# A two-layer decoder with routed experts on one core: another opening of the first expert products

## The chip, the core and the metric

The kernel runs on one core of one Trainium2 chip. TensorE (PE) multiplies, VectorE (DVE), ScalarE (ACT) and GpSimd (POOL) work element by element, SyncE (SP) and the queues of ScalarE and GpSimd issue DMAs. Every engine takes its instructions in the order in which they stand in the program; between engines, semaphores make one wait for another. The metric is the time of one execution on the device in microseconds (us); lower is better.

## What is computed

There are two layers over 256 tokens of width 1024. Each mixes tokens (attention in windows, a short convolution, a spatial gate) and then sends every token through PEER, a mixture of 128 x 128 experts of one neuron each. Only the second half matters here:

```python
q = (t @ w_pq).reshape(T, PEER_HEADS, 2, PEER_HALF)
s = jnp.einsum('thpk,hpnk->thpn', q, sub_keys)
top_s, top_i = lax.top_k(s, PEER_TOPK)                # 16 of 128 keys, twice for each of 8 heads
cand_s = top_s[:, :, 0, :, None] + top_s[:, :, 1, None, :]
best_s, best_pos = lax.top_k(cand_s.reshape(T, PEER_HEADS, 256), PEER_TOPK)
experts = jnp.take_along_axis(cand_i.reshape(T, PEER_HEADS, 256), best_pos, axis=-1)
gate = jax.nn.softmax(best_s, axis=-1)
act = jax.nn.gelu(jnp.einsum('td,thkd->thk', t, expert_down[experts]))
return jnp.einsum('thk,thkd->td', gate * act, expert_up[experts])
```

A token thus chooses 8 x 16 = 128 of 16384 experts.

## The kernel before, and its profile in words of the code

**Two ways to the same result.** The first T tokens of a layer (DENSE: 168 in layer 0, 160 in layer 1) are computed densely: each of 128 chunks of `down` (512 KB, 128 x 1024 f32) is multiplied with all T tokens on TensorE, the result goes through Gelu and is weighted with a gate matrix that is zero but for the chosen experts; then 128 chunks of `up` are multiplied and summed. The last 256 - T tokens (88 and 96) are computed by rows: for each token one indirect DMA from GpSimd's queue (`fetch`, L1038) gathers its 128 rows of `down` (512 KB again), VectorE multiplies them with the token (`dot`, L1048), and later the same is done with its rows of `up` (`add_row`, L1063). Rows are laid out by sets of tokens: 64, 16 and 8 tokens in layer 0, 64 and 32 in layer 1; each set needs the expert numbers and the token's values spread over the partitions (`spread_picks` into `pairs`, `dot_spread` into R_DX), and `where` (L1030, VectorE) turns the spread numbers into row addresses.

**The first products.** `experts` runs a loop over the 128 `down` chunks, numbered from 0. In the same loop stand, by a budget per chunk (`run_fill`), the steps of the choice on VectorE. They come for two halves of 128 tokens: first half 1 (tokens 128 to 255, which holds the tokens computed by rows), then half 0. The steps of a half are top-16 of the keys (`top_keys`), candidate sums (`cand`), top-16 of these (`top_cand`), `ranks`, three steps that turn positions into key numbers (`match`, `times`, `total`), `gate` (the softmax, with its Exp on ScalarE) and for half 1 `choose`, which writes `chosen`. When a half is known, `to_picks` transposes its results on TensorE (L918) and copies them on. The chunk at which half 1 is known is `begin` (11 in layer 0); the spreads and `where` are put at fixed lags behind it. After the second picks, `start`, the gate matrices are made (`compare` on VectorE, `factors` on ScalarE, `gate_mm` on TensorE).

**Buffers.** Chunks go through a ring of 7 buffers (`raw`), sent half by SP and half by ScalarE's queue. Ten chunks of a layer (AHEAD_AT) are sent early to free places of a large array (`arena`). Six more buffers hold chunks of the next modulation matrix (`aside`), which VectorE multiplies between other work. A row fetch needs a free place too: some fixed ones, and the seven of PASSING, which held early chunks before and are given up (`retired`) when the choice of half 0 nears its end, since results will lie there. Every `dot` frees the place of its row and fetches the next. DOT_SLOW and DOT_RATE are dots per chunk, before and after `start`. All DMAs of GpSimd's queue use eight semaphores in turn, so that one waits for the landing of the eighth before it.

**Lines.** L345 is a chunk's matmul of the first products, L1137 of the second, L1143 adds the rows' sums; L918 transposes picks, L926 copies them; L905 is the Exp, L906 to L908 the rest of the gate; L1020 and L1025 are the spreads.

Of the kernel before, what the change touches and what calls it, by code (L numbers as in the profile page):

```python
# [77 lines left out]
def hybrid_trunk(ctx: ExitStack, tc: tile.TileContext, x_in, c_in, vec_in, w_ada, w_in, w_out, w_pq,  # L78
# [37 lines left out]
    for n, t in enumerate(DENSE):  # L116
        for off, m in token_sets(S - t):
            nc.vector.tensor_reduce(fold[n][:, off:off + m], ident.rearrange("p (g n) -> p n g", n=m), op=OP.add,
                                    axis=AX.X)
    x_dram = dram.tile([P, DC * S], F32, name="x_dram")  # L120
# [39 lines left out]
    SLOTS_OPEN = [region(at * S, D) for at in (96, 100, 104)]  # L160
# [22 lines left out]
    class Src:  # L183
# [6 lines left out]
        asides = deque()  # L190
        ring = []
# [25 lines left out]
    def ada_chunk(layer, col, raw):  # L217
# [3 lines left out]
        if layer == 0 and col < G1:  # L221
            n = 1
        if (col + 1) % n == 0:
# [7 lines left out]
    def load_more(k):  # L231
        while Src.loaded < len(Src.seq) and (Src.ring[Src.loaded + 1] == Src.ring[Src.loaded]
# [75 lines left out]
    for layer in range(DEPTH):  # L308
# [3 lines left out]
        if layer == 0:  # L312
# [8 lines left out]
            body += mix(tail[:6], ada(0, [5])) + tail[6:]  # L321
        else:
            body += tail
# [8 lines left out]
        un = mix(un, aside[len(ASIDES_AT[layer]):], 4, 100)  # L332
# [490 lines left out]
    def retrieval(layer, update, late):  # L823
# [21 lines left out]
        tmp = R_PK[:, 3:6, :]  # L845
        sel = R_PK[:, 6:9, :]
# [6 lines left out]
        narrowed = R_TE[:, 0, 0].rearrange("p j i k -> p (j i k)")[:, :256].rearrange("p (h j i) -> p h j i", h=8, j=2)  # L853
# [47 lines left out]
        def gate():  # L901
# [3 lines left out]
            nc.scalar.activation(sel[:, 2, :], sel[:, 2, :], AF.Exp)  # L905
            nc.vector.tensor_reduce(red[:, :8], g, op=OP.add, axis=AX.X)  # L906
# [8 lines left out]
        def to_picks(b):  # L915
            ps = bank("g", 2)
            for j in range(3):
# [4 lines left out]
            high = tmp[:, 0, :].bitcast(F16)[:, :P]  # L922
# [30 lines left out]
        for d in range(DC):  # L953
            nc.scalar.activation(R_HX[:, d, :], R_H[:, d, :], AF.Identity, bias=shifts[:, d:d + 1])
        for pair in range(1, 8):
# [8 lines left out]
        def rest():  # L964
            scores(7)
            for b in (1, 0):
# [423 lines left out]
```

## Time and profile before

| what | value |
| --- | --- |
| three runs, median (lowest to highest) | 1617.16 us (1615.1 to 1618.89) |
| the profiled execution, its span | 1619.4 us, 1617.7 us |
| TensorE, VectorE, ScalarE, GpSimd busy | 96%, 62%, 29%, 32% |
| moved by DMA, mean rate | 570.27 MB, 353 GB/s |
| row fetches (L1038), all four forms | 368 |
| placing of sets by GpSimd, L1025 and L1020 | 32 and 32 DMAs |

The profile is one execution. A row of its views gives an engine, a line of the kernel, an operation, what it writes and reads, and in brackets how long the engine stood idle before it and what ended that. A row of the table by windows gives, for a stretch of time, the busy time of each engine with its count of instructions, TensorE's granted clock, the share of the DMA engines that was busy, and the GB/s that they moved. A chunk's product is 16 records of matmul in the profile, eight instructions in the program.

### The profile page before, as it was taken

The numbers are of one execution on the slowest core, as the hardware profiler recorded it, in microseconds if no ns is written. First come the engines' busy times: TensorE is split into PE (matmuls) and PEld (weight loads), VectorE is DVE, ScalarE is ACT, GpSimd is POOL, SyncE is SP. The second block draws the span as 40 slices with busy tenths as digits, with TensorE's granted clock in tenths as the row PEclk, the third lists the DMA queues.
The fourth block names the chain that finished last, engine by engine and source line by source line (L and its number), as shares of the span: only waits on it lengthen the run. The fifth ranks groups of instructions, "written<-read, shape, count | busy, mean of one in ns | idle before, by whom it ended". The sixth has DMA issues, their size and how long they took to land.

```text
span 1617.7 us, 29030 instructions
## 1 busy us (share of the span) xinstructions
PE 1550.2 (96%) x11240; PEld 1514.8 (94%) x11240; DVE 1002.7 (62%) x2263; ACT 475.4 (29%) x1356; POOL 518.5 (32%) x467
## 2 busy tenths in 40 slices
PE   7999996999999999998979999989999999999996
PEld 6879996999999999998979899989999999999995
DVE  6778884777777444444436668859777754444435
ACT  2346311466654000000015763115655510000000
POOL 1000125533333544444400001145433444444441
PEclk9999998999999999999979999989999999999997
DMA  9998647999999999999955666499999999999995
GB/s 387 344 361 310 184 151 254 360 419 418 419 418 418 418 419 419 418 419 418 420 216 169 195 231 198 149 387 374 419 418 418 418 419 419 419 419 418 418 419 201
DMA packets 157082, 570.27 MB, mean 353 GB/s; under 512 B 18736, under 2 KB 19312, under 8 KB 155792
## 3 DMA queue, kind: packets, MB, share of 16 engines
q1 hardware_dynamic: 65232, 237.92, 38.4%
q0 software_dynamic: 56144, 201.41, 31.3%
q10 hardware_dynamic: 35568, 129.08, 20.2%
q8 instruction: 88, 1.44, 0.3%
q14 instruction: 50, 0.41, 0.1%
HBM read 562.39 MB, written 3.15 MB: 350 GB/s over the span
## 4 chain that ended last, share of the span: by engine, by line
DMA 41%; PE 35%; issue 11%; POOL 6%; DVE 4%; ACT 2%; POOLq 0%; ACTq 0%; SPq 0%; DVEq 0%
DMA arena<-in_up,arena 28%; PE ch L345 18%; DMA spots<-in_up,arena 6%; POOL arena L1038 5%; DMA arena<-in_down_rows,arena 4%; PE ch L347 2%; PE ch L348 2%; PE ch L349 2%; DMA spots<-in_down_rows,arena 1%; DMA raw<-in_w_ada 1%; PE acc L1143 1%; POOL spots L1038 1%; DVE spots L1063 1%; PE ch L434 1%; PE g L936 1%
## 5 line engine op out<-in xcount | busy, mean ns | idle before, releaser
L345 PE MATMUL ch<-arena,raw 128*128 128x168 f32 (+2 forms) x3936 | 590.1, 309 | 8.2 <-issue 6.3
L1137 PE MATMUL acc<-arena,raw 128*128 128x168 f32 (+1 forms) x4096 | 581.0, 305 | 9.0 <-DMA raw<-in_up 9.0
L1137 PEld LDWEIGHTS acc<-arena,raw 128*128 128x128 f32 x4096 | 578.4, 192 | 11.0 <-DMA raw<-in_up 10.9
L345 PEld LDWEIGHTS ch<-arena,raw 128*128 128x128 f32 x3936 | 563.9, 192 | 15.5 <-issue 9.6
L1063 DVE SCALAR_TENSOR_TENSOR spots<-arena,spots 128x1024 f32<-128x1024 f32 x157 | 201.6, 1284 | 264.0 <-DMA arena<-in_up,arena 263.6
L1038 POOL DMA_INDIRECT arena<-in_up,arena x159 | 220.7, 1388 | 276.6 <-DMA arena<-in_up,arena 222.5
L1038 POOL DMA_INDIRECT arena<-in_down_rows,arena x148 | 163.1, 1102 | 240.1 <-DVE arena L1048 212.5
L1048 DVE SCALAR_TENSOR_TENSOR arena<-arena,spots 128x1024 f32<-128x1024 f32 x148 | 179.8, 1222 | 92.4 <-DMA arena<-in_down_rows,arena 90.7
L1081 ACT ACTIVATE arena<-arena,parts 128x128 f16<-128x128 f16 x164 | 64.6, 394 | 121.5 <-DVE arena L1071 81.2
L1114 ACT ACTIVATE arena<-ch 128x320 f32<-128x320 f32 (+30 forms) x122 | 42.0, 344 | 167.6 <-PE ch L345 141.7
L376 ACT ACT_TABLE_LOAD x6 | 7.7, 1283 | 264.5 <-PE acc L1137 264.4
L347 PE MATMUL ch<-hh,hi 128*128 128x256 f32 x288 | 82.6, 289 | 2.0 <-DVE arena L465 1.9
L348 PE MATMUL ch<-hh,lo 128*128 128x256 f32 x288 | 81.8, 284 | 0.0
L349 PE MATMUL ch<-hh,hi 128*128 128x256 f32 x288 | 81.7, 284 | 0.0
L258 DVE TENSOR_TENSOR lo<-raw,hi 128x1024 fp32r<-128x1024 f32 x42 | 51.2, 1224 | 24.0 <-ACT hi L265 23.8
L1038 POOL DMA_INDIRECT spots<-in_down_rows,arena x36 | 43.9, 1218 | 67.0 <-DVE spots L1048 47.9
L345 PE MATMUL ch<-arena 128*128 128x160 f32 (+2 forms) x384 | 62.7, 323 | 1.7 <-ACT arena L398 1.5
L218 DVE SCALAR_TENSOR_TENSOR raw<-raw,arena 128x1024 f32<-128x1024 f32 x48 | 57.8, 1215 | 9.1 <-DMA raw<-in_w_ada 5.5
L1087 ACT ACTIVATE arena<-arena,parts 128x128 f16<-128x128 f16 x164 | 63.4, 387 | 0.0
L1083 ACT ACTIVATE arena<-arena,parts 128x128 f16<-128x128 f16 x164 | 63.4, 387 | 0.0
L1085 ACT ACTIVATE arena<-arena,parts 128x128 f16<-128x128 f16 x164 | 63.4, 387 | 0.0
L345 PEld LDWEIGHTS ch<-arena 128*128 128x128 f32 x384 | 57.8, 194 | 6.0 <-ACT arena L398 4.0
(227 smaller groups left out, 1716.7 us busy)
## 6 DMA issues: line engine op xcount, KB each, us to landing
raw<-in_up SPq DMA_DIRECT2D x128, 512.0 KB
raw<-in_up ACTq DMA_DIRECT2D x128, 512.0 KB
raw<-in_down SPq DMA_DIRECT2D x118, 512.0 KB
raw<-in_down ACTq DMA_DIRECT2D x118, 512.0 KB
raw<-in_w_ada SPq DMA_DIRECT2D x48, 512.0 KB
aside<-in_w_ada SPq DMA_DIRECT2D x48, 512.0 KB
raw<-in_w_pq SPq DMA_DIRECT2D x32, 512.0 KB
raw<-in_w_in SPq DMA_DIRECT2D x26, 512.0 KB
```

Source lines behind the costliest of these rows:

```text
L345: nc.tensor.matmul(dst, hi[:, cols], k[0], start=start, stop=stop, **kw)
L347: nc.tensor.matmul(dst, hi[:, cols], k[0], start=start, stop=False, **kw)
L348: nc.tensor.matmul(dst, lo[:, cols], k[0], start=False, stop=False, **kw)
L349: nc.tensor.matmul(dst, hi[:, cols], k[1], start=False, stop=stop, **kw)
L1038: nc.gpsimd.indirect_dma_start(out=held[n], out_offset=None, in_=rows if n >= TS else down_rows[:, :], in_offset=bass.IndirectOffsetOnAxis ...
L1048: nc.vector.scalar_tensor_tensor(row, row, 1.0, R_DX[which(k)[0]], op0=OP.mult, op1=OP.mult, accum_out=R_DOTS[:, k:k + 1])
L1063: nc.vector.scalar_tensor_tensor(R_SUM[s], row, w, R_SUM[s], op0=OP.mult, op1=OP.add)
L1081: nc.scalar.activation(og[0][:, 0, i, :], oh[:, 0, i, :], AF.Copy, scale=parts[:, 0, t + i:t + i + 1])
L1083: nc.scalar.activation(og[1][:, 0, i, :], oh[:, 0, i, :], AF.Copy, scale=parts[:, 1, t + i:t + i + 1])
L1085: nc.scalar.activation(og[0][:, 1, i, :], oh[:, 1, i, :], AF.Copy, scale=parts[:, 0, t + 2 + i:t + 3 + i])
L1087: nc.scalar.activation(og[1][:, 1, i, :], oh[:, 1, i, :], AF.Copy, scale=parts[:, 1, t + 2 + i:t + 3 + i])
L1137: nc.tensor.matmul(acc[d // 2][:, (d % 2) * S:(d % 2) * S + T], u[:, d * P:(d + 1) * P], acts[:, i, :], start=i == 0 and d % 2 == 0, stop= ...
```

## The change

It is made in the opening of the first products, in both layers.

- *More early chunks.* AHEAD_AT has 15 places instead of 10. Three of the new ones (64, 68, 100) are free when the last scores are made, two (28, 32) when the keys of half 1 have their top-16; `Src.limits` holds the loading back until then. The list of choice results in `narrow` and the half-precision copy of the gates (R_HIGH) move to free places.
- *More rows ahead.* The place of every early chunk from the fourth on becomes a place for a row, from the chunk at which it is used; 100 stays one for good, the rest are given up as before. `where` of the first set comes three chunks after `begin` instead of four, and stands ahead of that chunk's choice steps.
- *Exponentials.* `exponents` (the subtraction and the Exp) is split off `gate` and stands before `ranks`.
- *Picks.* Their second copy goes to ScalarE; the subtraction for the low parts comes one chunk later (`lower`).
- *Small sets.* Instead of one DMA per group of partitions (48 in layer 0, 8 in layer 1), `spread_rest` writes `chosen` and the dot rows to memory and reads them back, spread, with three DMAs per set. `where` of the small sets comes 22 chunks after `begin` instead of 17, and stands behind the picks in the loop.
- *Dots, then gates.* DOT_SLOW is 0.3 instead of 0.2, DOT_RATE of layer 0 is 0.85 instead of 0.8; when the choice is done and `start` hasn't come, 1.6 dots go with each chunk. The gates begin six chunks after `start` instead of four.
- *Asides.* Six are sent in one go behind the early chunks.

```diff
-WHERE_LAG = 4
-SETS_LAG = (0, 6, 11)
-SETS_KNOWN = 17
+LOWER_LAG = 1
+WHERE_LAG = 3
+SETS_LAG = 6
+SETS_KNOWN = 22
-DOT_SLOW = 0.2
-DOT_RATE = (0.8, 0.92)
+DOT_SLOW = 0.3
+DOT_RATE = (0.85, 0.92)
+DOT_FAST = 1.6
-AHEAD_AT = (8, 12, 16, 36, 40, 44, 48, 52, 56, 60)
-PASSING = (36, 40, 44, 48, 52, 56, 60)
+AHEAD_AT = (8, 12, 16, 36, 40, 44, 48, 52, 56, 60, 64, 68, 100, 28, 32)
+KEPT = 100
+FLUSH = 6
+FIRST_LOWER = 1
-ASIDES_AT = ((16, 18, 19, 20, 22) + tuple(range(46, 127, 5)), (16, 17, 18, 19, 20, 21, 60, 72))
+ASIDES_AT = ((20,) * 6 + tuple(range(46, 125, 5)), (20,) * 6 + (60, 72))
...
-    SLOTS_OPEN = [region(at * S, D) for at in (96, 100, 104)]
+    SLOTS_OPEN = [region(at * S, D) for at in (96, 104)]
...
-        def gate():
+        def exponents():
             bv = best.rearrange("p (h k) -> p h k", h=8)
             g = sel[:, 2, :].rearrange("p (h k) -> p h k", h=8)
             nc.vector.tensor_sub(g, bv, bv[:, :, 0:1].to_broadcast([P, 8, 16]))
             nc.scalar.activation(sel[:, 2, :], sel[:, 2, :], AF.Exp)
+
+        def gate():
+            g = sel[:, 2, :].rearrange("p (h k) -> p h k", h=8)
             nc.vector.tensor_reduce(red[:, :8], g, op=OP.add, axis=AX.X)
...
-            nc.vector.tensor_copy(at[:, :, 0, :], ps[:, 0:P].rearrange("p (g t) -> p g t", t=4))
-            nc.vector.scalar_tensor_tensor(parts[:, 1, t], g, GATE_SCALE, high,
-                                           op0=OP.mult, op1=OP.subtract)
+            nc.scalar.copy(at[:, :, 0, :], ps[:, 0:P].rearrange("p (g t) -> p g t", t=4))
+            return lambda: nc.vector.scalar_tensor_tensor(parts[:, 1, t], g, GATE_SCALE, high, op0=OP.mult,
+                                                          op1=OP.subtract)
...
+        def spread_rest():
+            nc.gpsimd.dma_start(pair_in[layer], chosen[T - P:, :, :])
+            nc.gpsimd.dma_start(dot_in[layer], R_DROW[:TS, :])
+            for s in range(1, len(SETS)):
+                off, n = SETS[s]
+                for c in range(2):
+                    src = pair_in[layer][off:off + n, c, :].rearrange("t (h k) -> h t k", k=n)
+                    nc.gpsimd.dma_start(pairs[:, c, off:off + n], src)
+                src = dot_in[layer][off:off + n, :]
+                src = bass.AP(tensor=src.tensor, offset=src.offset, ap=[[0, P // n]] + list(src.ap))
+                nc.gpsimd.dma_start(R_DX[s], src)
...
+            n = i - AHEAD_FIRST
+            if 0 <= n < len(AHEAD_AT) and AHEAD_AT[n] >= 28:
+                assert not retired
+                free.append(region(AHEAD_AT[n] * S, D))
+                if AHEAD_AT[n] != KEPT:
+                    passing.append(free[-1])
+                fetch()
...
-                for s in range(1, len(SETS)):
-                    if i == begin + SETS_LAG[s]:
-                        spread_picks(s)
-                        dot_spread(s)
+                if i == begin + SETS_LAG:
+                    spread_rest()
...
-                    due += DOT_SLOW if start is None else DOT_RATE[layer]
+                    due += DOT_RATE[layer] if start is not None else DOT_SLOW if fills[0] else DOT_FAST
```

How the order changes shows at three places of layer 0. First GpSimd, from the spread of the first set on (`spots` holds the spread dot rows, the fetches write to `arena`); before:

```order
L1020 DMA spots<-spots 64x1024 x2
L1025 DMA pairs<-chosen 64x2x64 x2
L1038 DMA arena<-in_down_rows,arena 128x1024 x9
L1025 DMA pairs<-chosen 16x2x16 x8
L1020 DMA spots<-spots 16x1024 x8
L1025 DMA pairs<-chosen 8x2x8 x16
L1020 DMA spots<-spots 8x1024 x16
L1038 DMA arena<-in_down_rows,arena 128x1024
```

and now:

```order
L1041 DMA spots<-spots 64x1024 x2
L1046 DMA pairs<-chosen 64x2x64 x2
L1071 DMA arena<-in_down_rows,arena 128x1024 x13
L1050 DMA pair_in_103<-chosen 88x256
L1051 DMA dot_in_105<-spots 88x1024
L1056 DMA pairs<-pair_in_103 128x1x16 x2
L1059 DMA spots<-dot_in_105 128x1x1024
L1056 DMA pairs<-pair_in_103 128x1x8 x2
L1059 DMA spots<-dot_in_105 128x1x1024
L1071 DMA arena<-in_down_rows,arena 128x1024 x5
```

Thirteen row fetches stand ahead of the small sets instead of nine, and the small sets are 8 DMAs instead of 48. Second VectorE, at the end of the choice of half 0; before (L1030 is `where`, L906 to L908 the gate, L926 the copy of the second picks):

```order
L894 TENSOR_TENSOR arena<-arena 128x2048
L1030 TENSOR_SCALAR arena<-pairs 128x16
L1030 TENSOR_SCALAR arena<-pairs 128x8
L898 TENSOR_TENSOR arena<-arena 128x8x128
L898 TENSOR_TENSOR arena<-arena 128x8x64
L898 TENSOR_TENSOR arena<-arena 128x8x32
L899 TENSOR_TENSOR arena<-arena 128x128
L1048 SCALAR_TENSOR_TENSOR arena<-arena,spots 128x1024
L904 TENSOR_TENSOR arena<-arena 128x128
L906 TENSOR_REDUCE arena<-arena 128x8
L907 RECIPROCAL arena<-arena 128x8
L908 TENSOR_TENSOR arena<-arena 128x128
```

and now (L922 to L924 are the gate, L943 the low parts, L1104 `compare`, L1063 `where`):

```order
L912 TENSOR_TENSOR arena<-arena 128x128
L1081 SCALAR_TENSOR_TENSOR arena<-arena,spots 128x1024
L922 TENSOR_REDUCE arena<-arena 128x8
L923 RECIPROCAL arena<-arena 128x8
L924 TENSOR_TENSOR arena<-arena 128x128
L1081 SCALAR_TENSOR_TENSOR arena<-arena,spots 128x1024 x5
L943 SCALAR_TENSOR_TENSOR parts<-g,arena 128x128
L1104 TENSOR_TENSOR arena<-iota_85,picks 128x1024 x2
L1063 TENSOR_SCALAR arena<-pairs 128x16
L1063 TENSOR_SCALAR arena<-pairs 128x8
L1081 SCALAR_TENSOR_TENSOR arena<-arena,spots 128x1024 x6
```

`where` of the small sets went from ahead of the last `total` to behind the picks, and six dots (L1081) stand between the last `total` and the picks where one did. Third SP, at the passage from the query weights to the first products; before:

```order
L204 DMA raw<-in_w_pq 128x1024 x3
L204 DMA raw<-in_down 128x1024 x4
L204 DMA aside<-in_w_ada 128x1024 x3
L204 DMA raw<-in_down 128x1024
L204 DMA aside<-in_w_ada 128x1024
L204 DMA raw<-in_down 128x1024
L204 DMA aside<-in_w_ada 128x1024
L204 DMA raw<-in_down 128x1024 x12
```

and now:

```order
L213 DMA raw<-in_w_pq 128x1024 x2
L213 DMA arena<-in_down 128x1024
L213 DMA raw<-in_w_pq 128x1024
L213 DMA raw<-in_down 128x1024 x2
L213 DMA arena<-in_down 128x1024 x4
L213 DMA raw<-in_down 128x1024
L213 DMA aside<-in_w_ada 128x1024 x6
L213 DMA raw<-in_down 128x1024 x13
```

Five early chunks (into `arena`) more stand ahead of the asides, which now go together.

More of the change, by code (lines that the diff above doesn't have):

```diff
@@ L119, in hybrid_trunk @@
                                     axis=AX.X)
+    pair_in = [dram.tile([S - t, 2, P], F32, name=f"pair_in{n}") for n, t in enumerate(DENSE)]
+    dot_in = [dram.tile([S - t, D], F32, name=f"dot_in{n}") for n, t in enumerate(DENSE)]
     x_dram = dram.tile([P, DC * S], F32, name="x_dram")
@@ L190, in hybrid_trunk @@
         asides = deque()
+        limits = []
+        starts = []
         ring = []
@@ L222, in ada_chunk, with ada_end @@
             n = 1
+        ada_end(layer, col, n)
+    def ada_end(layer, col, n):
         if (col + 1) % n == 0:
@@ L231, in load_more @@
     def load_more(k):
-        while Src.loaded < len(Src.seq) and (Src.ring[Src.loaded + 1] == Src.ring[Src.loaded]
+        while Src.loaded < min([len(Src.seq)] + Src.limits) and (Src.ring[Src.loaded + 1] == Src.ring[Src.loaded]
                                              or Src.ring[Src.loaded] <= Src.ring[k + 1] + RAW - 2):
@@ L331, in hybrid_trunk @@
             dn.insert(at, aside[n])
-        un = mix(un, aside[len(ASIDES_AT[layer]):], 4, 100)
+        if layer + 1 < DEPTH:
+            un = mix(un, aside[len(ASIDES_AT[layer]):], *ASIDES_UP)
+        Src.starts.append(len(seq))
         seq += dn + un
@@ L954, in retrieval @@
             nc.scalar.activation(R_HX[:, d, :], R_H[:, d, :], AF.Identity, bias=shifts[:, d:d + 1])
+        Src.limits = [Src.starts[layer] + AHEAD_FIRST + n for n in (10, 13)]
         for pair in range(1, 8):
@@ L965, in rest @@
             scores(7)
+            Src.limits.pop(0)
             for b in (1, 0):
@@ L972, in rest @@
                     fill.append((0.3, narrow))
+                if b == 1:
+                    fill.append((0.0, lambda: Src.limits.clear()))
                 fill.append((0.95, lambda b=b: cand(b)))
@@ L975, in rest @@
                     fill.append((3.8, lambda h=h: top_cand(range(h, h + 4))))
+                fill.append((0.3, exponents))
                 fill.append((2.0, ranks))
@@ L980, in rest @@
                     fill.append((1.6, lambda j=j: total(j)))
-                fill.append((1.0, gate))
+                fill.append((0.7, gate))
                 if b == 1:
@@ L999, in experts @@
         beyond = [region(at * S, D) for at in (80, 84) if at * S >= P * T]
-        passing = [region(at * S, D) for at in PASSING]
-        free = deque([spots[:, n, :] for n in range(len(SETS), 3)] + [region(108 * S, D)] + beyond + passing)
+        passing = []
+        free = deque([spots[:, n, :] for n in range(len(SETS), 3)] + [region(108 * S, D)] + beyond)
         held = {}
@@ L1188, in experts @@
         known_at = []
+        lower = []
         shown = 0
@@ L1218, in experts @@
             if i == 0:
+                for n in range(min(FIRST_LOWER, len(fills[0]))):
+                    fills[0].popleft()[1]()
                 rest()
@@ L1223, in experts @@
                 dot_spread(0)
+            if begin is not None and i == begin + WHERE_LAG:
+                where(0)
+                known_to[0] = SETS[0][1]
+                fetch()
             if start is None:
@@ L1230, in experts @@
                     spread_picks(0)
+            while lower and lower[0][0] <= i:
+                lower.pop(0)[1]()
             while known_at and known_at[0][0] <= i:
-                known_at.pop(0)[1]()
+                lower.append((i + LOWER_LAG, known_at.pop(0)[1]()))
                 shown += 1
-            if start is None and shown == 2:
+            if start is None and shown == 2 and not lower:
                 start = i + 1
@@ L1241, in experts @@
                 free.extend(SLOTS_OPEN)
-            elif start is not None and i >= start + 4:
-                want = min(NG, -(-NG * (i - 3 - start) // (G_LAST - 4 - start)))
+            elif start is not None and i >= start + FLUSH:
+                want = min(NG, -(-NG * (i - FLUSH + 1 - start) // (G_LAST - FLUSH - start)))
                 if want < NG and i % 2:
@@ L1253, in experts @@
                     free.remove(row)
[L1254 to L1262 removed]
+            n = i - AHEAD_FIRST
[4 more added lines that the diff above has]
+                    passing.append(free[-1])
+                fetch()
+            if begin is not None:
+                if i == begin + SETS_LAG:
+                    spread_rest()
                 if i == begin + SETS_KNOWN:
```

20 lines of the change are left out of this document (8 added, 12 removed).

## The prediction

> **What bounds the kernel now.** I read the stages first, as a table of busy time by window, for layer 0's first products (about 200 to 524 us) and second products (524 to 826):
>
> ```profile
> core 0: us, PE busy (x) PEld busy (x) DVE busy (x) ACT busy (x) POOL busy (x), PEclk, DMA share, GB/s
> 200.00:221.00 21.00, 21.00 (x149) 21.00 (x148) 14.86 (x58) 4.52 (x8) 0.00 (x0) 1.00 0.31 95
> 221.00:231.40 10.40, 10.40 (x76) 10.40 (x75) 10.40 (x71) 1.87 (x6) 1.21 (x3) 1.00 0.43 116
> 231.40:260.00 28.60, 25.11 (x171) 24.37 (x170) 25.47 (x119) 2.71 (x6) 12.63 (x16) 1.00 0.95 363
> 260.00:280.00 20.00, 11.18 (x77) 10.61 (x75) 2.83 (x7) 1.73 (x2) 17.05 (x33) 0.84 0.56 145
> 280.00:300.00 20.00, 18.16 (x113) 18.15 (x114) 14.48 (x30) 9.05 (x26) 15.12 (x16) 0.81 0.85 260
> 300.00:524.00 224.00, 224.00 (x1753) 222.17 (x1752) 162.81 (x311) 127.83 (x448) 80.45 (x73) 1.00 1.03 418
> 524.00:826.00 302.00, 291.68 (x2015) 289.81 (x2013) 138.02 (x142) 2.06 (x4) 125.31 (x91) 0.99 1.03 418
> ```
>
> From 300 to 826 the DMA engines are full: 418 GB/s, so one 512 KB transfer (a chunk or a row fetch) costs 524,288 B / 418 GB/s = 1.25 us, and the layer ends when the last byte is in. TensorE still loses 302 − 291.7 = 10.3 us to that in the last of these rows. Before 300 the engines move 95 to 363 GB/s: the opening wastes the resource that is short later. Next the timeline of TensorE in that opening:
>
> ```profile
> 199.52 22.96 PE L345 MATMUL ch<-arena 128*128 128x168 f32 x160
> ...
> 222.65 18.12 PE L345 MATMUL ch<-arena,raw 128*128 128x168 f32 x126
> ...
> 244.19 8.99 PE L345 MATMUL ch<-arena,raw 128*128 128x168 f32 x62 [1.00 <-issue]
> ...
> 270.43 0.27 PE L918 MATMUL g<-ident,arena 128*128 128x128 f32 x1
> 279.18 0.48 PE L918 MATMUL g<-ident,arena 128*128 128x128 f32 x1 [8.48 <-DVE arena L899]
> 281.84 0.45 PE L918 MATMUL g<-ident,arena 128*128 128x128 f32 x1 [2.19 <-DVE arena L908]
> 282.08 16.47 PE L345 MATMUL ch<-arena,raw 128*128 128x168 f32 x96
> ```
>
> Ten chunks take 22.96 us, 2.30 each. TensorE then stands 8.48 + 2.19 = 10.7 us at the second picks (L918), behind VectorE. Why VectorE is late shows on its own timeline, and on GpSimd's:
>
> ```profile
> 220.07 0.28 DVE L906 TENSOR_REDUCE arena<-arena 128x8 f32<-128x128 f32 x1 [5.39 <-ACT arena L905]
> ...
> 230.92 0.17 DVE L1030 TENSOR_SCALAR arena<-pairs 128x64 uint32<-128x64 f32 x1
> ...
> 264.66 0.17 DVE L1030 TENSOR_SCALAR arena<-pairs 128x16 uint32<-128x16 f32 x1 [5.36 <-DMA spots<-spots]
> 277.25 0.17 DVE L1030 TENSOR_SCALAR arena<-pairs 128x8 uint32<-128x8 f32 x1 [12.41 <-DMA pairs<-chosen]
> ...
> 281.40 0.29 DVE L908 TENSOR_TENSOR arena<-arena 128x128 f32<-128x128 f32 x1
> ```
>
> ```profile
> 242.84 0.58 POOL L1025 DMA_DIRECT2D pairs<-chosen  x1
> ...
> 260.22 0.50 POOL L1025 DMA_DIRECT2D pairs<-chosen  x1 [3.70 <-DMA arena<-in_down_rows,arena]
> ...
> 285.06 2.00 POOL L1038 DMA_INDIRECT arena<-in_down_rows,arena  x1 [0.77 <-DVE arena L1071]
> ```
>
> From 242.8 to 285.1 us GpSimd is held by 48 small DMAs that place the two small sets, many behind an earlier landing (3.70 us in the middle row); no row is fetched meanwhile. VectorE stands 5.36 + 12.41 = 17.8 us in `where` for them, with the second picks queued behind. In layer 1 the small set is one, of 32, and that wait is absent:
>
> ```profile
> 1310.00:1584.00 274.00, 274.00 (x2018) 273.78 (x2017) 114.07 (x99) 0.92 (x3) 125.99 (x90) 1.00 1.03 419
> ```
>
> ```profile
> 1019.77 15.38 PE L345 MATMUL ch<-arena 128*128 128x160 f32 x112
> ...
> 1037.16 0.49 PE L918 MATMUL g<-ident,arena 128*128 128x128 f32 x3
> ...
> 1089.92 0.49 PE L918 MATMUL g<-ident,arena 128*128 128x128 f32 x3
> ...
> 1599.86 6.61 PE L1143 MATMUL acc<-fold,spots 128*128 128x32 f32 x30 [11.93 <-DVE spots L1063]
> ```
>
> There TensorE and DMA are both full up to 1584, and at the end TensorE waits 11.93 us for row sums that came last through DMA.
>
> **The change part by part.** Sums are against the profiled execution, 1619.4 us (span 1617.7); the median shown, 1617.16, is 2.2 lower.
>
> *Layer 0, second picks.* `where` of the small sets moves behind the picks (diff, order), and 48 DMAs become 8. The 17.8 us leave VectorE's path to L908, which would then have ended at 281.7 − 17.8 = 263.9. The order puts three dots ahead of the gate instead of two (one more is 1.2 us: 265.1); TensorE asks at 270.4. So what is late next is TensorE's own chunk, and 10.7 us go. After the wait it ran slow: 96 records in 16.47 us against 96 × 22.96/160 = 13.8, at a clock of 0.81; with no idle stretch ahead 2.7 more go. Together **13.4 us**.
>
> *Five more chunks and more rows ahead.* (Chunks are counted from 0.) Five chunks load while 95 GB/s flow (200 to 221). That alone only moves bytes; it counts where the program holds more at the same chunk later, when the engines are full. A row is fetched when a place is free, and each dot frees one. To the end of chunk 50 of layer 0: before, 9 places + 21 dots − 7 places given up + 3 opened + 1 (R_DROW) = 27 rows; after, 14 + 26 − 11 + 2 + 1 = 32. With one aside more held (6 against 5) that is 6 transfers, 6 × 1.25 = **7.5 us**. Layer 1: before 11 + 23 − 7 + 3 + 1 = 31, after 16 + 27 − 11 + 2 + 1 = 35: 4 × 1.25 = **5.0 us**, taken off the 11.93 at the end. Is there room? First rows start about 10 us earlier: the 5.39 us in which the gate stood for its exponentials go (they are sent five chunks sooner), and `where` of the first set stands two rounds of top-16 earlier and no longer behind the copy of the picks, so 230.92 becomes about 221 (at worst, if the pieces land late, 231 as now). From 221 to the end of chunk 40, eight chunks after the second picks and so near 289, 68 us hold 54 transfers; 24 rows, some 23 chunks, an aside and about 3 for placing are 51. It fits.
>
> *Costed at nothing.* The picks' copy of 128x128 goes from VectorE to ScalarE, which is busy 1.87 of 10.4 us there; the two table switches per exponential stay. Six asides are sent after the early chunks, in idle queues. The round trip writes the dot rows to memory, 0.36 MB, under 1 us a layer; uncovered it would cost that.
>
> *What stays.* Between the two picks lie 19 chunks, 19 × 2.30 = 43.6 us, and they took 270.4 − 222.65 = 47.8: 4.2 us are lost in gaps put to "issue", after nine row fetches in a burst (the 1.00 us ahead of the 244.19 row is one). In layer 1, 20 chunks × 15.38/7 = 43.9 took 1089.9 − 1037.5 = 52.4: 8.5 lost. No row shows a burst of 13 or 16; I keep the loss as it is, since the nearest rows are these two, with bounds from nothing (−12.7 us) to doubled (+12.7).
>
> Sum: 13.4 + 7.5 + 5.0 = 25.9; 1619.4 − 25.9 = 1593.5, less 2.2: **1591**.
>
> **The rivals.** *B, the gaps go too.* Raw buffers already hold chunks ahead while the rows burst, so TensorE runs through: 1591 − 12.7 = 1578. For it: more chunks wait in memory. Against: the gaps hit when DMA filled, and it will fill harder. A page bears on it: the Trainium skill, "Runtime: NRT & Kernel Launch", Instruction fetch mechanics, says that engines fetch instructions ahead over DMA and that this is mostly hidden; by it no such gap would exist, and this trace disagrees by the 1.00 us put to issue at 244.19.
>
> *C, the lead is worth nothing.* The extra rows only stand in the queue, dots wait longer on VectorE, and bytes arrive as before: 1591 + 12.5 = 1604. For it: from 300 on there is never a spare byte. Against: the spare bytes are before 300.
>
> *E, no earlier picks.* VectorE is late again because its faster dots wait for rows; 13.4 us return: 1605. Margin against it: 270.4 − 265.1 = 5.3 us.
>
> *D, slower: the placing lands late.* It now hangs on a write to memory behind 13 (layer 1: 16) row fetches. If those land 3.70 us apart from 221 on, as the 260.22 row waited, the write passes at 269; eight DMAs at 3.70 + 0.50 each end at 303. VectorE would stand in `where` from chunk 33, with the compares behind it; TensorE needs the first after chunk 40, near 289, and would lose 14 + 2.7 us. Layer 1, 16 rows from about 1034: 1093, six DMAs to 1118, needed after chunk 42, near 1107: 11 + 2.7. 1591 + 30 = 1621. It decides from the point where the last piece lands after 289. Against it: until chunk 19 is done, near 236, hardly a chunk buffer comes free, so rows have the engines almost alone, at 1.25 us. The Trainium skill, "DMA: Bandwidth & Descriptors", Anatomy of one DMA, gives about 2.0 us fixed per DMA, most of it confirmation by the memory written: by that page write and read together are an estimated 4 us, the placing is done near 250, and D falls away. No run here shows such a round trip.
>
> **How the numbers follow.** Forecast A 0.50 (1591), B 0.16 (1578), C 0.14 (1604), E 0.08 (1605), D 0.08 (1621), and 0.04 for parts of D that cancel the gain. Range 1575 to 1610: below B by the error of counting leads, above E by uncovered placing; only D and half of the cancelling lie outside by much. 0.2% (3.2 us) is about what a measurement of this kernel can tell from no change. Faster 0.88 (A, B, C, E), same 0.04, slower 0.08.
>
> **What would show it.** Right: no wait of TensorE at the second picks, nor of VectorE in `where`; the first row fetch near 221 and none of the 48 placing DMAs; over 200 GB/s from 260 to 280; layer 0's row sums done some 20 us sooner; under 8 us at TensorE's last wait. Wrong: a stand of VectorE in `where` of small sets, issue gaps of over 10 us after the first burst, or row sums ending where they did relative to the second products' start.

## The result, and the profile after

| | before | after |
| --- | --- | --- |
| median (lowest to highest) | 1618.03 us (1615.1 to 1619.04) | 1590.68 us (1589.67 to 1596.89) |
| ratio of after to before, 95% interval | | 0.9842 [0.9813, 0.9871] |
| the profiled execution, its span | 1619.4, 1617.7 us | 1591.52, 1589.7 us |
| layer 1's first matmul on TensorE starts at | 849.46 us | 827.69 us |

The changed kernel is 1.6% faster. One execution of e9 below took 1818 us at a granted clock of 0.858 and is left out of its ratio; every other execution in this document lies within 0.5% of its kernel's median. The rows that part the gain by layer are TensorE's first ones of layer 1 (257 columns wide), of before:

```profile
849.46 4.50 PE L434 MATMUL ch<-arena,raw 128*128 128x257 f32 x20
```

and of after, with TensorE's last wait in layer 1 below it:

```profile
827.69 4.50 PE L446 MATMUL ch<-arena,raw 128*128 128x257 f32 x20
...
1572.71 5.75 PE L1176 MATMUL acc<-fold,spots 128*128 128x32 f32 x30 [4.24 <-DVE spots L1096]
```

Layer 0 ends 849.46 − 827.69 = 21.8 us sooner; the span is 28.0 shorter, so layer 1 gives 6.2. The wait at the end went from 11.93 to 4.24 us.

Layer 0 has a wait at its end too, which the prediction's table of stages, ending at 826, cuts off. VectorE's last addition of a row in layer 0 and TensorE's sums of the rows (L1143), before:

```profile
831.78 1.29 DVE L1063 SCALAR_TENSOR_TENSOR spots<-arena,spots 128x1024 f32<-128x1024 f32 x1 [1.06 <-DMA arena<-in_up,arena]
833.12 9.55 PE L1143 MATMUL acc<-fold,spots 128*128 128x8 f32 x44 [8.47 <-DVE qg L523]
```

and after:

```profile
797.42 1.28 DVE L1096 SCALAR_TENSOR_TENSOR spots<-arena,spots 128x1024 f32<-128x1024 f32 x1 [1.53 <-DMA arena<-in_up,arena]
812.80 7.40 PE L1176 MATMUL acc<-fold,spots 128*128 128x64 f32 x48
```

Before, TensorE stood 8.47 us for the last rows (the L523 that is named is a small instruction right behind the last addition). After, the rows are done 34.4 us sooner (the prediction asked for some 20), and 14.1 us before TensorE asks for them. This wait, the 10.7 us at the second picks and the 2.7 us of slow clock behind them make 21.9 us, about what the layer gains (21.8); smaller terms of both signs stand beside them (the gaps cost 2.2 us more, waits for chunks in the second products 1.1 less).

The stages of layer 0's first products, after (busy time of each engine by window, then clock, DMA share, GB/s):

```profile
200.00:221.00 21.00, 21.00 (x150) 21.00 (x149) 20.28 (x96) 5.13 (x8) 1.19 (x2) 1.00 0.77 267
221.00:231.40 10.40, 9.63 (x68) 9.39 (x67) 7.44 (x50) 1.25 (x5) 7.87 (x9) 1.00 0.78 252
231.40:260.00 28.60, 25.48 (x164) 25.12 (x164) 26.44 (x101) 5.58 (x9) 14.08 (x16) 0.94 0.98 323
260.00:280.00 20.00, 20.00 (x141) 19.77 (x140) 10.22 (x22) 6.46 (x22) 4.35 (x3) 1.00 1.00 371
280.00:300.00 20.00, 20.00 (x152) 19.91 (x150) 14.15 (x28) 6.18 (x21) 8.51 (x7) 1.00 1.01 401
300.00:524.00 224.00, 224.00 (x1748) 222.04 (x1747) 164.21 (x307) 122.14 (x436) 90.15 (x77) 1.00 1.03 417
```

DMA moves 267 and 252 GB/s where it moved 95 and 116, and 371 and 401 where it moved 145 and 260. From 260 to 524 TensorE is never idle. Its timeline, and below it GpSimd's, in the opening:

```profile
230.48 0.30 PE L357 MATMUL ch<-arena 128*128 128x168 f32 x1 [0.15 <-issue]
231.88 0.30 PE L357 MATMUL ch<-arena 128*128 128x168 f32 x1 [1.10 <-issue]
...
272.99 0.49 PE L934 MATMUL g<-ident,arena 128*128 128x128 f32 x3
273.31 18.41 PE L357 MATMUL ch<-arena,raw 128*128 128x168 f32 x128
```

```profile
221.09 1.05 POOL L1071 DMA_INDIRECT arena<-in_down_rows,arena  x1 [3.58 <-DVE arena L840]
...
235.82 0.93 POOL L1071 DMA_INDIRECT arena<-in_down_rows,arena  x1 [2.45 <-remote]
...
240.03 0.62 POOL L1050 DMA_DIRECT2D pair_in<-chosen  x1
...
246.71 1.30 POOL L1056 DMA_DIRECT2D pairs<-pair_in  x2 [5.51 <-DMA pair_in<-chosen]
...
249.58 0.59 POOL L1059 DMA_DIRECT2D spots<-dot_in  x1
```

The second picks (272.99) have no wait. The first row is fetched at 221.09 (231.38 before), and the small sets are placed in eight DMAs, the last issued at 249.58. The gaps put to "issue" are still there, and larger.

### The profile page after: what moved, and what is told of

It is laid out like the page before. It is cut to its first block, busy times and chain, and to the rows that moved or that the text cites. A ratio compares the mean times of both kernels' runs of the same rounds, so it can differ in the third digit from the quotient of the medians.

```text
span 1589.7 us, 28955 instructions
## 1 busy us (share of the span) xinstructions
PE 1544.5 (97%) x11240; PEld 1509.4 (95%) x11240; DVE 998.3 (63%) x2255; ACT 472.6 (30%) x1356; POOL 498.5 (31%) x424
## 4 chain that ended last, share of the span: by engine, by line
PE 64%; DMA 27%; DVE 4%; issue 2%; ACT 2%; SPq 0%; DVEq 0%; ACTq 0%; POOLq 0%
PE ch L357 33%; DMA arena<-in_up,arena 17%; PE acc L1170 15%; DMA raw<-in_up 5%; DMA arena<-in_down_rows,arena 2%; PE ch L359 2%; PE ch L360 2%; PE ch L361 2%; PE g L1130 2%; DVE raw L227 1%; DMA raw<-in_w_ada 1%; PE ch L446 1%; PE g L952 1%; PE acc L1176 1%; DMA raw<-in_down 1%
## 5 line engine op out<-in xcount | busy, mean ns | idle before, releaser
L1170 PEld LDWEIGHTS acc<-arena,raw 128*128 128x128 f32 x4096 | 579.5, 192 | 10.3 <-DMA raw<-in_up 10.2
L357 PE MATMUL ch<-arena,raw 128*128 128x168 f32 (+2 forms) x3776 | 559.9, 307 | 1.1 <-DMA raw<-in_down 1.1
L357 PEld LDWEIGHTS ch<-arena,raw 128*128 128x128 f32 x3776 | 535.0, 190 | 6.9 <-issue 2.0
L1071 POOL DMA_INDIRECT arena<-in_up,arena x159 | 217.0, 1365 | 276.4 <-DMA arena<-in_up,arena 208.9
L1071 POOL DMA_INDIRECT arena<-in_down_rows,arena x151 | 176.2, 1167 | 247.9 <-DVE arena L1081 184.3
L1081 DVE SCALAR_TENSOR_TENSOR arena<-arena,spots 128x1024 f32<-128x1024 f32 x151 | 182.2, 1221 | 46.7 <-DMA arena<-in_down_rows,arena 34.8
L1147 ACT ACTIVATE arena<-ch 128x336 f32<-128x336 f32 (+32 forms) x122 | 42.7, 350 | 255.3 <-PE ch L357 217.6
L357 PE MATMUL ch<-arena 128*128 128x160 f32 (+2 forms) x544 | 90.3, 324 | 13.5 <-issue 11.5
L357 PEld LDWEIGHTS ch<-arena 128*128 128x128 f32 x544 | 83.6, 199 | 19.2 <-issue 13.0
L227 DVE SCALAR_TENSOR_TENSOR aside<-aside,arena 128x1024 f32<-128x1024 f32 x48 | 58.6, 1222 | 37.4 <-DMA aside<-in_w_ada 37.4
L1140 DVE SCALAR_TENSOR_TENSOR arena<-arena,g 128x336 f32<-128x336 f32 (+30 forms) x82 | 40.3, 492 | 56.3 <-ACT arena L1138 43.6
```

The source lines that it names most:

```text
L227: nc.vector.scalar_tensor_tensor(raw, raw, 1.0, cact, op0=OP.mult, op1=OP.mult, accum_out=mods[layer][:, col:col + 1])
L357: nc.tensor.matmul(dst, hi[:, cols], k[0], start=start, stop=stop, **kw)
L1071: nc.gpsimd.indirect_dma_start(out=held[n], out_offset=None, in_=rows if n >= TS else down_rows[:, :], in_offset=bass.IndirectOffsetOnAxis ...
L1081: nc.vector.scalar_tensor_tensor(row, row, 1.0, R_DX[which(k)[0]], op0=OP.mult, op1=OP.mult, accum_out=R_DOTS[:, k:k + 1])
L1170: nc.tensor.matmul(acc[d // 2][:, (d % 2) * S:(d % 2) * S + T], u[:, d * P:(d + 1) * P], acts[:, i, :], start=i == 0 and d % 2 == 0, stop= ...
```

## The experiments

All results side by side. "Layer 1 opens" and "the rest" are read from the profiled execution: the start of TensorE's first row of layer 1, and the span from there on. "Picks" is the time on TensorE from the first picks to the second in layer 0 and in layer 1. Without a gap the 19 and 20 chunks between take 43.65 and 43.80 us, so what is above that is gap; 1.20 us of it in layer 0 of before and 0.97 in layer 1 of after are a wait for a chunk, and e1's 45.2 is a lower clock, without an idle row. A trace is one execution: that of e10 is 3.3 us shorter than the median beside it, those of e4 and e9 3.5 shorter, those of e1, e2 and e11 6.2, 5.4 and 2.2 longer, so differences of two traces can be off by as much. The runs were made in three groups, e1 to e4, e5 to e8 and e9 to e12, each group on one chip with its own runs of before (1620.2, 1615.7 and 1619.8 us), so kernels of different groups are compared by their ratios. These too differ by chip: e3 and e9 are one kernel, and their ratios are 0.0018 (2.9 us) apart.

| kernel | median us | ratio to before [95%] | layer 1 opens | the rest | picks |
| --- | --- | --- | --- | --- | --- |
| before | 1618.0 | | 849.5 | 768.2 | 48.1, 52.8 |
| after | 1590.7 | 0.9842 [0.9813, 0.9871] | 827.7 | 762.0 | 50.3, 55.8 |
| e1 before, `where` late | 1606.9 | 0.9919 [0.9903, 0.9936] | 848.7 | 762.7 | 45.2, 45.3 |
| e2 e1 and placing through memory | 1605.3 | 0.9898 [0.9868, 0.9928] | 836.4 | 772.6 | 43.7, 43.8 |
| e3 after, 10 early chunks | 1588.5 | 0.9808 [0.9790, 0.9825] | 824.0 | 762.8 | 43.7, 43.8 |
| e4 after, old placing | 1594.0 | 0.9846 [0.9829, 0.9862] | 830.1 | 758.7 | 43.7, 43.8 |
| e5 after again | 1588.8 | 0.9832 [0.9814, 0.9851] | 824.7 | 762.3 | 50.1, 55.2 |
| e6 before again | 1618.4 | | 848.9 | 767.8 | 47.8, 52.5 |
| e7 after, shifted | 1589.3 | 0.9840 [0.9819, 0.9860] | 824.1 | 762.6 | 50.1, 55.7 |
| e8 after, rows one by one | 1585.4 | 0.9801 [0.9778, 0.9823] | 822.6 | 761.5 | 45.6, 47.4 |
| e9 as e3 | 1591.3 | 0.9826 [0.9799, 0.9853] | 821.8 | 764.3 | 43.7, 43.8 |
| e10 after a third time | 1586.3 | 0.9796 [0.9779, 0.9812] | 819.8 | 761.4 | 43.7, 43.8 |
| e11 after, placed twice | 1595.6 | 0.9847 [0.9831, 0.9864] | 827.9 | 768.0 | 43.7, 43.8 |
| e12 after, rows late | 1602.0 | 0.9890 [0.9873, 0.9906] | 830.9 | 769.1 | 43.7, 43.8 |

**e1: is the stand at the second picks worth its 13.4 us?**

```diff
-SETS_KNOWN = 17
+SETS_KNOWN = 22
```

> The kernel before, with one number changed: where of the small sets 22 chunks after begin instead of 17, so behind the second picks; the 48 placing DMAs stay. Theory 1 (TensorE's stand at the second picks cost 13.4 us by itself): about 1604.6 us, 13.4 below before, no wait of TensorE at the second picks of layer 0. Theory 2 (the layer ends with its last byte, so the stand only counted for the transfers that it held back): TensorE's stand goes but at most half of it is gained, 1611 to 1618.

Measured: 1606.9, 13.1 us below before. That is theory 1's number, but not by its path. TensorE's timeline in layer 0:

```profile
270.40 0.51 PE L918 MATMUL g<-ident,arena 128*128 128x128 f32 x3
...
306.68 0.58 PE L1097 MATMUL g<-arena 128*128 128x128 f16 x2 [11.16 <-ACT arena L1081]
```

The picks no longer wait, but ten chunks later the third gate matmuls (L1097) wait 11.16 us for ScalarE's factors, which need the compares, and these stand on VectorE behind `where`. The stand has moved to the next consumer. Layer 1 opens hardly sooner (848.7), and the rest takes 762.7 us instead of 768.2, with no gap in either layer. But this trace has a granted clock of 0.942, where that of before has 0.978, and took 1613.1 us, so the gain can't be divided between the layers by it; e2 shows more.

**e2: does GpSimd hold back the rows?** The kernel of e1, and `spread_rest` of the change at begin + 6, in place of the spreads at begin + 6 and + 11.

```diff
-                for s in range(1, len(SETS)):
-                    if i == begin + SETS_LAG[s]:
-                        spread_picks(s)
-                        dot_spread(s)
+                if i == begin + SETS_LAG:
+                    spread_rest()
```

> The kernel before with where of the small sets behind the second picks and the small sets placed through memory, 8 DMAs instead of 48 in layer 0. Theory 1 (rows are held back by places and dots, not by GpSimd): the same as with the late where alone, within 2 us. Theory 2 (GpSimd, held by 48 DMAs from 243 to 285 us, kept rows from being fetched): 5 us or more below the late where alone.

Measured: 1605.3, 1.6 us below e1 by the medians, with overlapping intervals; theory 2's 5 us are not shown, and the runs of e2 (1598.6 to 1610.7) are too far apart to exclude them. Placing through memory alone does not free the opening: VectorE still stands in `where`, as its timeline shows,

```profile
282.04 0.17 DVE L1044 TENSOR_SCALAR arena<-pairs 128x8 uint32<-128x8 f32 x1 [7.91 <-DMA pairs<-pair_in]
```

and TensorE stands 7.92 us in layer 0 and 11.41 us in layer 1 at its third gates. Still layer 1 opens 13.1 us sooner than in the trace of before: from 199 us to there TensorE's idle stretches of 0.4 us and more add up to 19.2 us instead of 31.3. Of these 3.65 us are for the row sums at the end of the layer, instead of 8.47, and none are gaps. The rest takes 4.4 us longer, with the 11.41 us in it. These two edits together gave 16 us; some 15 more came from the others (e2 to e3, by their ratios on one chip).

**e3 and e9: fewer early chunks and places.**

```diff
-AHEAD_AT = (8, 12, 16, 36, 40, 44, 48, 52, 56, 60, 64, 68, 100, 28, 32)
+AHEAD_AT = (8, 12, 16, 36, 40, 44, 48, 52, 56, 60)
...
-    SLOTS_OPEN = [region(at * S, D) for at in (96, 104)]
+    SLOTS_OPEN = [region(at * S, D) for at in (96, 100, 104)]
```

> The changed kernel with 10 early chunks and 9 first row places as before, all else as changed. Theory 1 (the lead is worth 1.25 us for each transfer): 12 us above the changed kernel, about 1603, of it some 7 us in layer 0 and 5 in layer 1. Theory 2 (lead worth nothing, rows only stand in the queue longer): within 2 us of the changed kernel. If the loss in TensorE's issue gaps grows with the length of the first burst of rows, it is back at about 4 us in layer 0 and 8 in layer 1 here.

Measured: 0.9808, at or below the changed kernel's 0.9842. Theory 1's 12 us are not there, for two reasons. The lead was counted wrong: in the program 29 rows are fetched by the end of chunk 50 of layer 0 and not 27, since two of the five rows come from the quicker dots, which stay. And this trace has no gaps, while that of after has 18.6 us of them, so the two could not be compared. e9 repeats it beside the changed kernel on one chip, where neither has gaps:

> The changed kernel with 10 early chunks and the old places again, now beside the changed kernel on one chip. Counted in the program, 29 rows are fetched by the end of chunk 50 of layer 0 instead of 32, and 31 instead of 35 in layer 1 (the other rows of the lead come from the quicker dots). Theory 1 (a row more in hand is 1.25 us): 3.75 + 5 = 8.75 us above the changed kernel of the next run, in traces without gaps put to issue; where there are gaps, less by what shorter gaps give back. Theory 2 (lead worth nothing): within 2 us in each layer, gaps or not.

Measured: 0.9826 against 0.9796 of e10, 4.9 us; in the profiles layer 1 opens 2.0 us later and the rest takes 2.9 longer. By these numbers both theories miss: three rows more are worth 2.0 us and four rows 2.9, about 0.7 us a row, half the price of a transfer. The size is not sure: the intervals of the two ratios overlap, and two of the three executions of e9 that count took 1587.8 us, 1.6 above e10's median. The traces show more than the times. In layer 0 VectorE ends the last row 8.4 us later in e9 (805.2 against 796.8), but TensorE asks at 808.5, so it waits for no row in either kernel. In layer 1 its wait for the rows at the end is 9.54 us instead of 5.40, 1.0 us for each of the four rows.

**e4: the old placing in the changed kernel.** `spread_rest` is replaced by the two spreads at their old lags, and SETS_KNOWN is 17.

```diff
-SETS_LAG = 6
-SETS_KNOWN = 22
+SETS_LAG = (0, 6, 11)
+SETS_KNOWN = 17
```

> The changed kernel with the small sets placed by 48 small DMAs at the old lags and where of the small sets 17 chunks after begin again. Theory 1 (this stand was worth 13.4 us): VectorE stands in where of the small sets for over 10 us, the picks come late, about 1604. Theory 2 (ScalarE copies the picks now, so VectorE may be late without TensorE standing): within 3 us of the changed kernel, 1588 to 1594.

Measured: 0.9846, between the theories if set against the 0.9842 of after; but this trace has no gaps, and against the changed kernel without gaps (e10, 0.9796) it is 8.1 us slower. TensorE's timeline:

```profile
273.66 0.48 PE L934 MATMUL g<-ident,arena 128*128 128x128 f32 x1 [6.47 <-DVE arena L912]
275.56 0.47 PE L934 MATMUL g<-ident,arena 128*128 128x128 f32 x1 [1.43 <-DVE arena L924]
275.83 21.28 PE L357 MATMUL ch<-arena,raw 128*128 128x168 f32 x128
```

The stand at the second picks is back, 7.9 us, and 128 records behind it take 21.28 us, at a granted clock of 0.86, where after takes 18.41 at 1.00: 10.8 us together. Layer 1 opens 830.1 − 819.8 = 10.3 us later (against a trace from another chip). So in layer 0 a stand in this place is paid nearly in full, with the slow clock behind it. In layer 1 it is not: VectorE stands 16.84 us in `where` and TensorE 3.40 + 1.58 us at the second picks, and yet the rest takes 2.7 us less than in e10.

**e5, e6, e7: whose are the gaps?** e5 and e6 are the changed kernel and the kernel before as they are; e7 adds instructions without use.

```diff
+SHIFT = 8
...
+    for _ in range(2):
+        ps = bank("g", 2)
+        for n in range(4):
+            nc.tensor.transpose(ps[:, n * P:(n + 1) * P], ident, ident)
+    for n in range(SHIFT):
+        nc.vector.memset(ones, 1.0)
+        nc.gpsimd.memset(ones, 1.0)
+        nc.scalar.activation(spare, eps, AF.Copy)
```

> The changed kernel once more, as it is. The gaps put to issue behind the first burst of rows stood in the traces of before (4.2 us in layer 0, 8.5 in layer 1) and of the change (6.4 and 11.6), and in none of the four kernels tried since. Theory 1 (they belong to the program: where its instructions lie): the same gaps again, 6 and 11 us, about 1590. Theory 2 (they belong to the chip or to the single execution): gone here, and the time 10 to 18 us lower, 1573 to 1580.

> The kernel before once more, one look. Theory 1 (the gaps belong to the program): the gaps of 4 and 8 us behind the first burst of rows again, near 1619. Theory 2 (they belong to the chip or the execution): none, about 1606.

> The changed kernel with eight instructions without use on each of TensorE, VectorE, ScalarE and GpSimd at the start, so that all later instructions lie elsewhere in the engines' streams. Theory 1 (the gaps depend on where the instructions lie): gaps of another size, perhaps none; without any, 10 to 18 us below the changed kernel, 1573 to 1580. Theory 2 (the gaps come from the 13 and 16 row fetches in one burst): the same gaps, within 3 us of the changed kernel.

Measured: the gaps of after (6.5 and 11.4 us) and of before (4.2 and 8.7) are back within 0.6 us of their first sizes, and the shifted kernel has them too (6.4 and 11.9):

```profile
230.95 0.45 PE L358 MATMUL ch<-arena 128*128 128x168 f32 x2 [0.44 <-issue]
232.39 0.45 PE L358 MATMUL ch<-arena 128*128 128x168 f32 x2 [0.99 <-issue]
234.50 0.45 PE L358 MATMUL ch<-arena 128*128 128x168 f32 x2 [1.67 <-issue]
```

So they are no accident of one execution, and moving the instructions by eight changes nothing. That is a small shift: a chunk's product on TensorE is eight instructions.

**e8: rows one by one.** Five rows are fetched at first, and one more with each chunk.

```diff
+BURST = 5
+BURST_UP = 1
...
-                known_to[0] = SETS[0][1]
+                known_to[0] = BURST
                 fetch()
+            elif begin is not None and begin + WHERE_LAG < i and known_to[0] < SETS[0][1]:
+                known_to[0] = min(SETS[0][1], known_to[0] + BURST_UP)
+                fetch()
```

> The changed kernel with 5 rows fetched when where has run and one more with each chunk, instead of all free places at once. Theory 2 (the gaps come from the burst): no gaps in either layer, and 10 to 18 us below the changed kernel, less what the later rows cost, 1575 to 1583. Theory 1 (the gaps depend on where the instructions lie): gaps that come or go whatever the burst; if they stay, 1590 to 1595.

Measured: 1585.4 (ratio 0.9801), 3.4 us below the changed kernel of the same group; gaps of 1.9 and 3.6 us (0.93 of these a wait for a chunk) instead of 6.5 and 11.4. The burst makes the gap long, and of the 12.4 us of gap that go, 3.4 show in the time. It is the fastest kernel of its group, but the intervals overlap by 0.0009.

**e10: the changed kernel once more, on the chip of e9, e11 and e12.**

> The changed kernel a third time, as the reference of its neighbours on this chip. If the gaps put to issue belong to the chip, they are there or not in all four kernels of this call alike; if they belong to the program, this one has them (6 and 11 us) and the one with 10 early chunks has none.

Measured: 1586.3, 0.9796, and no gaps, as in its three neighbours and in all four of e1 to e4:

```profile
221.97 0.49 PE L934 MATMUL g<-ident,arena 128*128 128x128 f32 x3
...
265.62 0.49 PE L934 MATMUL g<-ident,arena 128*128 128x128 f32 x3
```

The same program has 18 us of gaps on one chip and none on another, so whether they come depends on the chip, or on something that went with the occasion (each group was one chip on one occasion); how long they are depends on the program, as before, after and e8 show. The changed kernel's ratio is 0.9832 − 0.9796 = 0.0036 better without them, some 6 us, and its time 2.6 us; before has gaps of its own, and its time is 4.1 us longer on e10's chip, so no run here gives the price of the gaps alone. What takes a part of that back on the chip without gaps stands on VectorE's timeline in layer 1:

```profile
1056.94 0.27 DVE L1063 TENSOR_SCALAR arena<-pairs 128x32 uint32<-128x32 f32 x1 [13.37 <-DMA pairs<-pair_in]
```

TensorE runs ahead there, so `where` of the small set comes before its pieces have landed, and TensorE then loses 2.84 us at 1065.45, behind ScalarE, which waits for VectorE's compares. In the trace with gaps `where` had no wait.

**e11: the small pieces twice.**

```diff
-                    nc.gpsimd.dma_start(pairs[:, c, off:off + n], src)
+                    for n_th in range(2):
+                        nc.gpsimd.dma_start(pairs[:, c, off:off + n], src)
```

> The changed kernel with the DMAs that read expert numbers and gates of the small sets back from memory issued twice: 512 more pieces of 64 and 32 bytes in layer 0, 256 of 128 bytes in layer 1. After the placing the DMA engines are fully busy but move only 200 to 330 GB/s for some 20 us, 2.7 MB less than 418 GB/s would. Theory 1 (the small pieces cost that): as much again, about 6 us in layer 0 and 3 in layer 1. Theory 2 (it is the token rows, read from memory 8 and 16 times over, or the write): within 2 us.

Measured: 0.9847 against 0.9796, 8.3 us slower; layer 1 opens 8.1 later and the rest takes 6.6 longer. The windows around the placing in e10,

```profile
250.00:260.00 10.00, 10.00 (x72) 10.00 (x71) 9.79 (x19) 1.21 (x3) 7.47 (x9) 1.00 0.94 279
260.00:270.00 10.00, 9.53 (x68) 9.30 (x67) 3.03 (x10) 2.93 (x11) 2.97 (x3) 1.00 1.02 341
270.00:280.00 10.00, 10.00 (x72) 10.00 (x71) 9.16 (x16) 4.45 (x15) 5.50 (x5) 1.00 1.03 421
```

and in e11:

```profile
250.00:260.00 10.00, 10.00 (x72) 10.00 (x71) 9.79 (x17) 1.36 (x3) 1.86 (x3) 1.00 0.91 306
260.00:270.00 10.00, 10.00 (x73) 10.00 (x72) 2.96 (x8) 2.15 (x7) 1.70 (x3) 1.00 0.89 226
270.00:280.00 10.00, 10.00 (x72) 10.00 (x71) 1.11 (x2) 5.56 (x19) 1.71 (x4) 1.00 0.88 297
```

In e10 the slump lasts 20 us: at a share of 1.02 the engines move 341 GB/s. Doubled, it is longer and deeper. Theory 2's bound of 2 us falls: reading the pieces of 32 to 128 bytes once more is dear. But the ways in which it costs are not parted here: GpSimd's busy time drops from 15.9 to 5.3 us over the three windows, as it waits on its queue and fetches no rows, so rows come late; and VectorE stands in `where` for 8.96 and 15.63 us, where e10 has none and 13.37. The Trainium skill, "DMA: Bandwidth & Descriptors", Specifications, names 512 bytes as the least transfer for full rate; that agrees in direction with the 341 GB/s. The old placing moved pieces of the same sizes, but straight from `chosen`; no run here compares the two.

**e12: rows late.** The exponentials are back in the gate, and `where` of the first set comes four chunks after `begin`, behind the choice steps.

```diff
-WHERE_LAG = 3
+WHERE_LAG = 4
...
-                fill.append((0.3, exponents))
...
-                fill.append((0.7, gate))
+                fill.append((1.0, lambda: (exponents(), gate())))
...
```

> The changed kernel with the exponentials back in the gate and where of the first set back in its old place, four chunks after begin and behind the choice steps, so that the first row fetch comes some 10 us later. Theory 1 (the early start makes the room for the lead): from the first fetch to the end of chunk 40 only 46 of 51 transfers fit, about 6 us slower in layer 0. Theory 2 (the start of the rows does not matter, there are bytes to spare until 300 us): within 2 us.

Measured: 0.9890 against 0.9796, 15.2 us slower, more than theory 1 asked for and the largest of the parts undone one at a time (it undoes two edits together). In the traces layer 1 opens 11.1 us later and the rest takes 7.7 longer. GpSimd's first row, and then VectorE's and TensorE's waits behind it:

```profile
229.56 1.05 POOL L1070 DMA_INDIRECT arena<-in_down_rows,arena  x1 [6.12 <-DVE arena L840]
```

```profile
272.88 0.18 DVE L1062 TENSOR_SCALAR arena<-pairs 128x16 uint32<-128x16 f32 x1 [2.75 <-DMA pairs<-pair_in]
283.27 0.17 DVE L1062 TENSOR_SCALAR arena<-pairs 128x8 uint32<-128x8 f32 x1 [10.21 <-DMA pairs<-pair_in]
...
1079.29 0.18 DVE L1062 TENSOR_SCALAR arena<-pairs 128x32 uint32<-128x32 f32 x1 [16.81 <-DMA pairs<-pair_in]
```

```profile
301.82 0.58 PE L1129 MATMUL g<-arena 128*128 128x128 f16 x2 [5.25 <-ACT arena L1113]
...
1087.81 8.28 PE L357 MATMUL ch<-arena,raw 128*128 128x160 f32 x48 [14.03 <-ACT arena L1146]
```

The rows start 9.2 us later than in e10 (220.37), the placing queues behind them on GpSimd, the pieces land late, and VectorE stands 13.0 us in `where` in layer 0 and 16.8 in layer 1. The compares, and with them ScalarE's factors and TensorE, wait behind it: 5.25 us at a gate in layer 0, and 14.03 us at a chunk in layer 1. Row sums are not what is late: in layer 0 they end at 805.2, and TensorE asks at 817.7. This is the chain that the prediction gave to its rival D.

## Why the prediction came out right, and which of its steps did not

The time came out as forecast (1591 against 1590.7), and so did the shares of the layers (20.9 and 5.0 us against 21.8 and 6.2). Its steps did less well; errors of both signs cancel, so that the total is this near is in part luck.

- **Layer 0, second picks, 13.4 us: the right wait, not the right edit.** No wait at the second picks, no 48 DMAs, no stand in `where`: all as listed. e4 gives the price of such a stand in layer 0: 10.3 us for a stand and slow clock of 10.8. But the step that took the 17.8 us off VectorE's path by moving `where` behind the picks was half a step: alone it only moves the stand to the third gates (11.16 us in e1, 7.92 in e2). It goes for good only where the pieces have landed when `where` comes.
- **First rows some 10 us earlier: the step that was missing.** The prediction used the early exponentials and the early `where` only to ask whether there is room for 51 transfers. e12 shows a term of their own, 15.2 us, when they come late again: rows that start early get out of the placing's way on GpSimd's queue.
- **Lead, 7.5 us in layer 0: the size came out by luck.** The step was that the layer ends when the last byte is in, so that each transfer in hand is worth 1.25 us. What went is the 8.47 us that TensorE stood for the last rows, and then the rows are 14.1 us early: the layer no longer ends with them. The early chunks are not what removed the wait, since in e9, without them, the rows still end before TensorE asks; e9 prices their three rows at 2.0 us. Two of layer 0's five rows come from the quicker dots, not from places. The two dots and the sixth aside were not tried alone.
- **Lead, 5.0 us in layer 1: right in kind.** Without the four rows TensorE's wait at the end is 4.1 us longer and the rest 2.9 (e9 against e10): 0.7 to 1.0 us a row instead of 1.25.
- **Gaps kept as they were, 12.7 us: they grew.** 4.5 and 9.0 us became 6.6 and 12.0 (the picks column less 43.65 and 43.80), inside the bounds given, but in layer 1 over the 10 us that the prediction named as a sign of being wrong. Of before's 4.5 us, 1.20 was a wait for a chunk (at 254.39), not a gap put to "issue". Rival B, in which they vanish, was put at 12.7 us below the forecast. On the chip without gaps the ratio gives 0.9796 × 1618 = 1585 rather than 1578. A reason that fits, though no run tests it: while TensorE stands in a gap, DMA goes on (393 GB/s from 230 to 236 in after, 405 in e5), and DMA is what is short later. The page cited there, "Runtime: NRT & Kernel Launch" of the Trainium skill, has instruction fetch mostly hidden; the two chips without gaps agree. On the others moving the instructions by eight changed nothing, so no run here makes the fetch the cause; a shift that small doesn't exclude it either.
- **Rival D: its mechanism is real, its place and price were off.** With the early rows the placing is issued by 249.58 in layer 0 (254.53 in e10), and `where` finds it landed. That is near the 250 of the estimate from the Trainium skill's page, but not by its 2 us for each DMA: behind the rows GpSimd waited 5.51 us in after and 13.39 us in e10 for the write to memory alone. With late rows D's chain appears and costs 15 us (e12), not 30. In layer 1 of e10 it stands on VectorE for 13.37 us and costs TensorE 2.84: the margin there is used up.
- **Placing costed at nothing.** "Under 1 us a layer" counted the bytes of the write. The wait for it was 5.51 and 13.39 us on GpSimd, and reading the small pieces once more costs some 8 us a run (e11), so the round trip is not free; its price alone was not measured.

The parts need not add up: undone one at a time, they take back 8, 5 and 15 us (e4, e9, e12) of the 33 us that e10 gains, while e1 and e2 gain 13 and 16 by themselves. They share the same in-order queues of VectorE and GpSimd, where one lateness can hide another. How the remaining gain divides between quicker dots, gates two chunks later and the sixth aside stays open.

## What to carry to other kernels

A wait that is removed from one consumer on an in-order engine comes back at the next consumer in line unless its producer also becomes earlier; look two consumers down before booking it. Where a long transfer queue stands ahead of a short, needed one on the same engine, the start of the long one is a term of its own. A lead is worth time only where its consumer is what is waited for: in layer 0 of the changed kernel the rows end before TensorE asks, with the extra early chunks or without, and in layer 1, where TensorE does wait for them, a row was worth 0.7 to 1.0 us and not 1.25.

## What the runs showed of the hardware

The gaps of TensorE and VectorE in the first burst of row fetches come on one chip and not on another, or on one occasion and not on another: with the same program 6.5 and 11.4 us (e5) and none (e10). They are the same within 0.6 us when repeated, unmoved by eight more instructions on each engine, and 1.9 and 3.6 us when the burst is thinned (e8). In the trace of after they begin some 9 us into the burst; GpSimd itself loses 2.45 us put to "remote" at 235.82. The DMA queues that the traces call "instruction" move a packet between 226 and 230 in after and in e10, and two more from 237 to 240 in after, from 230 to 237 in e10; that neither shows nor excludes that instructions come late. What starves the engines is not shown by any run.

While pieces of 32 to 128 bytes are read among rows and chunks (250 to 270 in e10, to 280 in e11), the DMA engines move 226 to 341 GB/s at shares of 0.88 to 1.02; from 300 to 524 in after, with chunks and rows, they move 417 at 1.03.

A write to memory behind a burst of row fetches on GpSimd's queue kept GpSimd waiting 5.51 us in after and 13.39 us in e10 until it had landed.
